# Sharing two groups of convolution channels between VectorE and ACT with GpSimd, tap by tap, in a two-layer speech encoder

## The chip, the cores and the metric

The kernel runs on one core of a Trainium2 chip. The metric is the device time of one execution in microseconds; the median of several runs is compared. A core has five engines that run their own queues in order and wait for each other through semaphores: TensorE (PE in the profile, its weight loads PEld), VectorE (DVE), ScalarE (ACT), GpSimd (POOL) and SyncE (SP), which here issues most of the transfers.

## The reference

Two layers of a Conformer-like block over 512 tokens of 1024 features, in float32. Each layer is a half-step feed-forward block, a mixing block, a second half-step feed-forward block and a norm:

```python
x = x + 0.5 * swiglu(rms_norm(x, ffn1_norm[l]), ...)
h = rms_norm(x, mix_norm[l])
p = h @ w_in[l]
attn = mla_group(p[..., :o_kv], p[..., o_kv:o_pe], p[..., o_pe:o_cv], ...)
conv = conv_group(p[..., o_cv:], conv_w[l], conv_b[l], conv_ln_g[l], conv_ln_b[l])
x = x + jnp.concatenate([attn, conv], axis=-1) @ w_out[l]
x = x + 0.5 * swiglu(rms_norm(x, ffn2_norm[l]), ...)
x = rms_norm(x, post_norm[l])
```

The attention has 8 heads with low-rank queries and keys and a block-causal mask. The convolution is the part that matters here; it has 512 channels, and each channel has a filter of its own with 31 taps over time:

```python
def conv_group(u_raw, conv_w, conv_b, ln_g, ln_b):
    a, g = u_raw[..., :CONV_W], u_raw[..., CONV_W:]
    u = a * jax.nn.sigmoid(g)
    y = lax.conv_general_dilated(u, conv_w[:, None, :], window_strides=(1,), padding=[(CONV_K - 1, 0)],
                                 feature_group_count=CONV_W)   # causal, depthwise
    y = y + conv_b
    return jax.nn.silu(layer_norm(y, ln_g, ln_b))              # norm over the 512 channels of a token
```

## The kernel before

Features lie on the 128 partitions and the 512 tokens along the free dimension, so the 512 convolution channels are four groups of 128, `c` = 0 to 3, each a tile of 128x512. A product of matrices is done as three matmuls of rounded parts (`mm3`, L153 to L157: high by high, high by low, low by high). The high part of a weight tile is a copy on ACT (L138) and the low part a subtraction on VectorE (L144); for the output weights `wo` of kind "sum" the low part is a copy of the negative on ACT (L141) and a transfer from GpSimd's queue that adds onto it (L142). `split` (L159) makes the two parts of an activation tile, the high one on ACT (L161), the low one on VectorE (L162).

The program is written in an order of its own, and a planner orders the instructions of each engine at build time by a timeline of its own (`schedule_with_timeline_sim=True`, L1237); the queues then run in that fixed order, however long things take. `tc.issue_after(i)` keeps an instruction behind `i` in that order.

`mix_body` (L617) is the mixing block. Its projections run on TensorE in the order of `SEQ` (L44): the inputs of channel group 0 come first, those of group 1 (`c1`) after the first part of the queries, those of groups 2 and 3 (`c2`, `c3`) last, behind the keys. `glu` (L624) forms `u[c]` out of them (VectorE L626, L630, L632, ACT L628). Queries and keys get their norms with a power on GpSimd (`rsqrt`, L173: `scq` for queries, `sck` for keys; `order["keys"]` is the last of the keys' four). Attention then goes head by head through `STAGES` (L889): transposes of queries and keys (L811 to L818), scores with their maxima on VectorE (L836) and exponentials on ACT (L840), transposes of the probabilities (L855, evicted at L858), sums and values (L870, L877), the product with the reciprocal sum (L880) and, per pair of heads, the split into `at`.

The convolution is written behind attention (L914 to L933), but its instructions are put between those of attention and of the projections. Before, a letter a group says who does it (`CONV = "DAAD"`, L41):

- "D", groups 0 and 3: an accumulator `acc` in PSUM (tag `cv`, one bank, so one group at a time) is started by ACT (L918, the newest tap and the bias), VectorE adds the 30 other taps, one instruction each (L922), and ACT copies the result back over `u[c]` (L932).
- "A", groups 1 and 2: an accumulator `ys[c]` in SBUF is started by ACT; for each of the 30 other taps ACT makes the product `pr` (L926, three buffers) and GpSimd adds it to the accumulator (L930). Additions with `s >= PAUSE` (16), and all of group 2, come behind `order["keys"]`.

Then follows the norm over channels: GpSimd sums the four groups into `ysum` (L944 to L946), a matmul with a constant tile averages over the channels (L948, `pm`), VectorE subtracts that mean from each group (L954), squares and sums follow (ACT L184 and L187, VectorE L191), a matmul adds the squares over channels (L198), GpSimd takes the power (L173), a matmul spreads the result (L217, `pr`), and VectorE and ACT scale, apply silu and split (L964, L966, L161, L162) into `cv`.

The output product has eight row blocks `m`, each a sum of four products with `at` and four with `cv` in one PSUM bank. The `at` part of the first three blocks (`early_groups`, 36 matmuls) needs no convolution and lies in the program behind the squares; the `cv` part of these three, and then the other blocks, follow at L970 to L980, behind which the second feed-forward block begins.

Tiles: `kept` (tag `m`, 12 buffers) holds the four `u`, the four value tiles and the first two `at` pairs; the other two pairs come from the ring of 35 buffers.

Of the kernel before, what the change touches and what calls it, by code (L numbers as in the profile page):

```python
# [7 lines left out]
FP = mybir.dt.float32  # L8
# [3 lines left out]
AF = mybir.ActivationFunctionType  # L12
ALU = mybir.AluOpType
AX = mybir.AxisListType

P = 128
D = 1024
S = 512
# [11 lines left out]
CK = 31  # L30
# [6 lines left out]
WIDE = 6  # L37
NP = 3
NC = 2
CHUNKS = ((0, 2), (2, 5), (5, 8), (8, 11))  # L40
CONV = "DAAD"  # L41
AHEAD = 2
PAUSE = 16
SEQ = "q0 R c1 q1 q2 qo k kt tt uq uk c2 c3"  # L44
# [3 lines left out]
EARLY = "s"  # L48
PRELOAD = 1
E1 = 0  # L50
YP = 1
E2 = 2
E3 = 3
WOG = 3
# [20 lines left out]
def encoder_kernel(ctx: ExitStack, tc: tile.TileContext, xT, consts, vecs, rgain, wgu1, wd1, wdq1,  # L75
# [8 lines left out]
    psum = ctx.enter_context(tc.tile_pool(name="psum", bufs=7, space=PSUM))  # L84
    uid = [0]

    def nm(s):
        uid[0] += 1
        return f"{s}{uid[0]}"
# [4 lines left out]
    def tmp(w=S, dt=FP):  # L94
        return tmps.tile([P, w], dt, tag="t", name=nm("t"))

    def bank():
        return psum.tile([P, S], FP, tag="ps", name=nm("ps"))
# [4 lines left out]
    V, A, G, T = nc.vector, nc.scalar, nc.gpsimd, nc.tensor  # L103
# [26 lines left out]
    def vv(l, name):  # L130
        o, w = VOFF[name]
        return vec[:, l, o:o + w]
# [18 lines left out]
    order = {}  # L151
# [7 lines left out]
    def split(src, made=slot):  # L159
        hi, lo = made(FR), made(FR)  # L160
        order["high"] = A.copy(hi, src).ins  # L161
        order["evicted"] = V.tensor_tensor(lo, src, hi.bitcast(FP), ALU.subtract).ins  # L162
        return hi, lo
# [46 lines left out]
    def spread(r):  # L210

        dg = tmp()
        V.tensor_tensor(dg.rearrange("p (t j) -> p t j", t=NT),
                        ident[:, None, :].to_broadcast([P, NT, P]),
                        r[:, :, None].to_broadcast([P, NT, P]), ALU.mult)
        ps = bank()
        order["spread"] = T.matmul(ps, ones, dg, start=True, stop=True).ins  # L217
        return ps
# [13 lines left out]
    def groups(srcs, rhs, ws=None):  # L232

        ws = ws or [load_w(src, WC) for src in srcs]
        os = [bank() for _ in srcs]
        for ks in (range(KD - 1), range(KD - 1, KD)):
            for o, w in zip(os, ws):
                group(o, w, rhs, ks, KD)
        return os
# [373 lines left out]
    def mix(l, gx, norm, done):  # L613
        with tc.tile_pool(name="k", bufs=4) as kpool:
            mix_body(kpool, l, gx, norm, done)

    def mix_body(kpool, l, gx, norm, done):  # L617
        u, order = [], {}

        def kept(dt=FP):  # L620
            return kpool.tile([P, S], dt, tag="m", name=nm("m"), bufs=2 * WIDE)
        ys = [None if kind == "D" else kpool.tile([P, S], FP, tag="y", name=nm("y"), bufs=2) for kind in CONV]

        def glu(pa, pg):  # L624
            tg = tmp()
            V.tensor_tensor(tg, pg, R, ALU.mult)  # L626
            sg = tmp()
            order["gate"] = A.activation(sg, tg, AF.Sigmoid).ins  # L628
            ta = tmp()
            V.tensor_tensor(ta, pa, R, ALU.mult)  # L630
            uc = kept()
            (G if GLUP else V).tensor_tensor(uc, ta, sg, ALU.mult)  # L632
            u.append(uc)
# [155 lines left out]
        first = groups([wcv[l, 0], wcv[l, 1]], gx)  # L789
# [12 lines left out]
        at = []  # L802
# [3 lines left out]
        heads = [{} for _ in range(H)]  # L806
# [76 lines left out]
        def turn_out(h):  # L883

            if h % 2 == 0:
                return
            at.append(split(heads[h]["o"], kept if len(at) < 2 else slot))

        STAGES = [({"t": turn, "s": scores, "p": turn_p, "v": values, "o": turn_out}[c], int(d)) for c, d in zip(ORDER[::2], ORDER[1::2])]  # L889

# [5 lines left out]
        with tc.issue_after(order["turned"]):  # L896
            for t in range(NT):
                ps = up_kv(wv, t)
                v = kept()
                V.tensor_scalar(v, ps, sk[:, t:t + 1], None, ALU.mult)  # L900
                vs.append(v)
        with tc.issue_after(order["gate"]):
            scores(0)
        for step in range(H + 6):
            for stage, lag in STAGES:
                h = step - lag
# [4 lines left out]
        with tc.issue_after(order["keys"]):  # L911
            wo = [load_w(wout[l, m], WC, "sum") for m in range(WOP)]
        cw, cb = vv(l, "cw"), vv(l, "cb")
        for c in range(4):  # L914
            kind = CONV[c]
            acc = psum.tile([P, S], FP, tag="cv", name=nm("cv"), bufs=1) if kind == "D" else ys[c]
            tap = lambda k: cw[:, c * CK + k:c * CK + k + 1]
            A.activation(acc, u[c], AF.Identity, scale=tap(CK - 1), bias=cb[:, c:c + 1])  # L918
            for k in range(CK - 2, -1, -1):
                s = CK - 1 - k  # L920
                if kind == "D":
                    V.scalar_tensor_tensor(acc[:, s:], u[c][:, :S - s], tap(k), acc[:, s:], ALU.mult, ALU.add)  # L922
                    continue
                pr = kpool.tile([P, S], FP, tag="pr", name=nm("pr"), bufs=3)
                if kind == "A":
                    A.activation(pr[:, s:], u[c][:, :S - s], AF.Copy, scale=tap(k))  # L926
                else:
                    G.tensor_scalar(pr[:, s:], u[c][:, :S - s], tap(k), None, ALU.mult)
                with tc.issue_after(order["keys"]) if s >= PAUSE or c > 1 else nullcontext():
                    order["conv"] = G.tensor_tensor(acc[:, s:], acc[:, s:], pr[:, s:], ALU.add).ins  # L930
            if kind == "D":
                A.copy(u[c], acc)  # L932
                ys[c] = u[c]  # L933
        early = []

        def early_groups(ms):
            with tc.issue_after(heads[H - 1][EARLY]):
                for m in ms:
                    early.append(bank())
                    group(early[m], wo[m], at, range(4), KD)  # L940

        early_groups(range(E1))
        ysum = tmp()
        G.tensor_tensor(ysum, ys[0], ys[1], ALU.add)  # L944
        G.tensor_tensor(ysum, ysum, ys[2], ALU.add)
        (G if YP else V).tensor_tensor(ysum, ysum, ys[3], ALU.add)  # L946
        pm = bank()
        T.matmul(pm, onesm, ysum, start=True, stop=True)  # L948
        if PRELOAD:
# [8 lines left out]
        pr = spread(r)  # L958
        early_groups(range(E3, WOG))
        lg, lb = vv(l, "lg"), vv(l, "lb")  # L960
        cv = []
        for c in range(4):
            z = tmp()
            V.tensor_tensor(z, ys[c], pr, ALU.mult)  # L964
            s = tmp()
# [275 lines left out]
```

## Time and profile before

| what | value |
|---|---|
| median of 3 runs | 1813.45 us (1812.57 to 1814.0) |
| profiled execution, its own time | 1813.8 us |
| its span, first to last instruction | 1812.0 us |
| mean granted TensorE clock | 0.995 |
| ACT busy | 1095.9 us (60%) |
| GpSimd (POOL) busy | 424.4 us (23%) |
| convolution taps of layer 0, first to last | 372.8 to 505.5 us of the span |
| convolution taps of layer 1 | 1270.6 to 1405.9 us |

In a row of a timeline the first number is the start in us from the span's beginning, the second the time the row covers in us, then engine, line, operation, the tile written and the tiles read, the shapes, and the number of instructions that the row merges; in brackets stand the idle time of the engine ahead of the row and what ended it. Rows of the table of waits give total us, number of waits and the longest. Rows of windows give, after the window and its length, the busy us of each engine with its number of instructions, then the granted clock, the busy share of the DMA engines and GB/s. A row of one source line gives the duration in ns as minimum, median and maximum. The recorded durations of neighbouring instructions on one engine overlap a little, so a busy time can reach the window's full length.

### The profile page before, as it was taken

The numbers are of one execution on the slowest core, as the hardware profiler recorded it, in microseconds if no ns is written. First come the engines' busy times: TensorE is split into PE (matmuls) and PEld (weight loads), VectorE is DVE, ScalarE is ACT, GpSimd is POOL, SyncE is SP. The second block draws the span as 40 slices with busy tenths as digits, with TensorE's granted clock in tenths as the row PEclk, the third lists the DMA queues.
The fourth block names the chain that finished last, engine by engine and source line by source line (L and its number), as shares of the span: only waits on it lengthen the run. The fifth ranks groups of instructions, "written<-read, shape, count | busy, mean of one in ns | idle before, by whom it ended". The sixth has DMA issues, their size and how long they took to land. (4 is left out here: it accounts for less than half of the span.)

```text
span 1812.0 us, 29094 instructions
## 1 busy us (share of the span) xinstructions
PE 1777.8 (98%) x11238; PEld 1582.1 (87%) x11238; DVE 1496.1 (83%) x2263; ACT 1095.9 (60%) x1729; POOL 424.4 (23%) x343
## 2 busy tenths in 40 slices
PE   9999999999989999999999999999999899999998
PEld 7899999888668899999888999998976788999997
DVE  7898988689946989898779989876999569989884
ACT  5565656467943575756645656554779435656564
POOL 1000000258843000000310000002688420000102
PEclk9999999999999999999999999999999999999999
DMA  5657574325103466665426575743260126575752
GB/s 167 165 135 190 125 183 114 108 88 140 24 16 107 121 165 160 153 156 133 123 64 169 127 188 124 191 108 115 74 152 1 37 86 165 135 180 134 177 121 73
DMA packets 70411, 226.14 MB, mean 125 GB/s; under 512 B 7936, under 2 KB 8320, under 8 KB 70272
## 3 DMA queue, kind: packets, MB, share of 16 engines
q1 hardware_dynamic: 54000, 169.74, 29.9%
q0 software_dynamic: 16128, 54.53, 17.6%
q8 instruction: 88, 1.44, 0.3%
q14 instruction: 51, 0.42, 0.1%
q10 hardware_dynamic: 144, 0.00, 0.0%
HBM read 222.15 MB, written 2.10 MB: 124 GB/s over the span
## 5 line engine op out<-in xcount | busy, mean ns | idle before, releaser
L155 PE MATMUL ps<-r,wh 128*128 128x256 f32 (+1 forms) x2540 | 806.1, 318 | 0.0
L154 PE MATMUL ps<-r,wh 128*128 128x256 f32 (+1 forms) x2540 | 803.4, 320 | 2.4 <-ACT wh L1060 0.9
L156 PE MATMUL ps<-r,wl 128*128 128x256 f32 (+1 forms) x2348 | 750.5, 321 | 1.9 <-DVE wl L246 1.9
L154 PEld LDWEIGHTS ps<-r,wh 128*128 128x128 f32 x2540 | 481.0, 189 | 45.0 <-ACT wh L138 3.1
L155 PEld LDWEIGHTS ps<-r,wh 128*128 128x128 f32 x2540 | 482.0, 190 | 34.3 <-issue 1.4
L156 PEld LDWEIGHTS ps<-r,wl 128*128 128x128 f32 x2348 | 445.2, 190 | 37.4 <-DVE wl L246 3.5
L373 PE MATMUL ps<-xj,wh 128*128 128x512 f32 x864 | 304.8, 392 | 4.6 <-DVE t L426 4.6
L138 ACT CAST wh<-raw 128x1024 fp32r<-128x1024 f32 (+3 forms) x148 | 131.8, 899 | 201.1 <-PE ps L155 101.8
L390 POOL DMA_DIRECT2D ls<-in_wgu x72 | 62.6, 869 | 733.0 <-ACT ls L389 640.2
L244 ACT CAST wh<-fr 128x1024 fp32r<-128x1024 f32 (+1 forms) x160 | 157.8, 986 | 109.4 <-DVE fr L410 47.8
L144 DVE TENSOR_TENSOR wl<-raw,wh 128x1024 fp32r<-128x1024 f32 (+3 forms) x132 | 145.3, 1108 | 83.2 <-ACT wh L138 82.7
L246 DVE TENSOR_TENSOR wl<-fr,wh 128x1024 fp32r<-128x1024 f32 (+1 forms) x160 | 182.8, 1142 | 20.5 <-ACT wh L244 20.5
L373 PEld LDWEIGHTS ps<-xj,wh 128*128 128x128 f32 x864 | 161.3, 188 | 36.3 <-DVE t L426 6.2
L930 POOL TENSOR_TENSOR y<-y,pr 128x511 f32<-128x511 f32 (+14 forms) x120 | 160.8, 1340 | 56.2 <-ACT pr L926 49.0
L374 PE MATMUL ps<-xj,ls 128*128 128x256 f32 x576 | 161.3, 280 | 0.0
L246 DVE TENSOR_TENSOR wl<-raw,wh 128x1024 fp32r<-128x1024 f32 (+1 forms) x100 | 113.8, 1138 | 14.8 <-ACT wh L244 14.4
L244 ACT CAST wh<-raw 128x1024 fp32r<-128x1024 f32 (+1 forms) x100 | 98.1, 981 | 44.9 <-PE ps L155 27.9
L191 POOL TENSOR_TENSOR r<-r,t 128x512 f32<-128x512 f32 x45 | 75.1, 1678 | 175.7 <-ACT t L187 174.9
L389 ACT ACTIVATE ls<-fr 128x1024 fp32r<-128x1024 f32 (+1 forms) x56 | 56.1, 1001 | 88.3 <-PE ps L374 49.6
L374 PEld LDWEIGHTS ps<-xj,ls 128*128 128x128 f32 x576 | 108.3, 188 | 0.2
L926 ACT ACTIVATE pr<-m,vec 128x511 f32<-128x511 f32 (+14 forms) x120 | 87.1, 752 | 11.3 <-POOL y L930 11.3
L390 POOL DMA_DIRECT2D ls<-in_wdq x32 | 27.6, 862 | 269.7 <-ACT ls L389 269.7
(241 smaller groups left out, 2967.4 us busy)
## 6 DMA issues: line engine op xcount, KB each, us to landing
fr<-in_wgu SPq DMA_DIRECT2D x112, 512.0 KB, 4.2
ls<-in_wgu POOLq DMA_DIRECT2D x72, 512.0 KB, 6.8
raw<-in_wgu SPq DMA_DIRECT2D x62, 512.0 KB, 5.1
fr<-in_wdq SPq DMA_DIRECT2D x48, 384.0 KB, 5.4
ls<-in_wdq POOLq DMA_DIRECT2D x32, 384.0 KB, 4.7
raw<-in_wd SPq DMA_DIRECT2D x32, 384.0 KB, 3.1
raw<-in_wd SPq DMA_DIRECT2D x32, 256.0 KB, 2.7
raw<-in_wcv SPq DMA_DIRECT2D x16, 512.0 KB, 3.6
```

Source lines behind the costliest of these rows:

```text
L138: order["cast"] = A.copy(hi[:, :w], raw[:, :w]).ins
L144: (G if kind in POOLW.split() else V).tensor_tensor(lo[:, :w], raw[:, :w], hi[:, :w].bitcast(FP), ALU.subtract)
L154: T.matmul(o, lh, rh, start=first, stop=False, skip_group_check=free)
L155: T.matmul(o, lh, rl, start=False, stop=False, skip_group_check=free)
L156: order["mm"] = T.matmul(o, ll, rh, start=False, stop=last, skip_group_check=free).ins
L244: A.copy(hi[:, :w], src[:, :w])
L246: order["lo"] = V.tensor_tensor(lo[:, :w], src[:, :w], hi[:, :w].bitcast(FP), ALU.subtract).ins
L373: T.matmul(o, w[0][:, c], both, start=start and k == 0, stop=False, skip_group_check=True)
L374: last = T.matmul(o[:, 0:HS], w[1][:, c], both[:, 0:HS], start=False, stop=k == 3, skip_group_check=True).ins
L390: G.dma_start(out=lo[:, :n], in_=w, accum_op=ALU.add)
L926: A.activation(pr[:, s:], u[c][:, :S - s], AF.Copy, scale=tap(k))
L930: order["conv"] = G.tensor_tensor(acc[:, s:], acc[:, s:], pr[:, s:], ALU.add).ins
```

## The change

`CONV` is replaced by `TAPS = (14, 17, 31, 0)`: for group `c` with `n = TAPS[c]`, the taps at distances 0 to n − 1 go to ACT and GpSimd in the SBUF accumulator `ys[c]`, the taps at distances n to 30 to VectorE in the PSUM accumulator `acc`. Group 2 stays wholly with ACT and GpSimd, group 3 wholly with VectorE; groups 0 and 1, which were whole on either side, are shared. Where a group is shared, ACT starts both accumulators (the PSUM one with the product of distance n) and VectorE joins them with one addition. The sum of the four groups moves from GpSimd to VectorE, one addition as each group is done, the last one reading group 3 in PSUM. The additions of distances below 16 of groups 0 and 1 are free to come ahead of the keys; distance 16 of group 1 and all of group 2 stay behind them. The second pair of attention outputs moves from `kept` (now 10 buffers) to the ring, and tag `y` has three buffers instead of two.

```diff
-CONV = "DAAD"
+TAPS = (14, 17, 31, 0)
...
-            return kpool.tile([P, S], dt, tag="m", name=nm("m"), bufs=2 * WIDE)
-        ys = [None if kind == "D" else kpool.tile([P, S], FP, tag="y", name=nm("y"), bufs=2) for kind in CONV]
+            return kpool.tile([P, S], dt, tag="m", name=nm("m"), bufs=10)
+        ys = [kpool.tile([P, S], FP, tag="y", name=nm("y"), bufs=3) if n else None for n in TAPS]
...
-            at.append(split(heads[h]["o"], kept if len(at) < 2 else slot))
+            at.append(split(heads[h]["o"], kept if len(at) < 1 else slot))
...
-        for c in range(4):
-            kind = CONV[c]
-            acc = psum.tile([P, S], FP, tag="cv", name=nm("cv"), bufs=1) if kind == "D" else ys[c]
+        ysum = None
+        for c, n in enumerate(TAPS):
             tap = lambda k: cw[:, c * CK + k:c * CK + k + 1]
-            A.activation(acc, u[c], AF.Identity, scale=tap(CK - 1), bias=cb[:, c:c + 1])
-            for k in range(CK - 2, -1, -1):
-                s = CK - 1 - k
-                if kind == "D":
-                    V.scalar_tensor_tensor(acc[:, s:], u[c][:, :S - s], tap(k), acc[:, s:], ALU.mult, ALU.add)
+            acc = psum.tile([P, S], FP, tag="cv", name=nm("cv"), bufs=1) if n < CK else None
+            first = dict(func=AF.Identity, scale=tap(CK - 1), bias=cb[:, c:c + 1])
+            if n:
+                A.activation(ys[c], u[c], **first)
+            for s in range(n or 1, CK):
+                k = CK - 1 - s
+                if s == n:
+                    A.activation(acc[:, s:], u[c][:, :S - s], AF.Copy, scale=tap(k))
                     continue
+                if s == 1 and not n:
+                    A.activation(acc, u[c], **first)
+                V.scalar_tensor_tensor(acc[:, s:], u[c][:, :S - s], tap(k), acc[:, s:], ALU.mult, ALU.add)
+            for s in range(1, n):
+                k = CK - 1 - s
                 pr = kpool.tile([P, S], FP, tag="pr", name=nm("pr"), bufs=3)
-                if kind == "A":
-                    A.activation(pr[:, s:], u[c][:, :S - s], AF.Copy, scale=tap(k))
-                else:
-                    G.tensor_scalar(pr[:, s:], u[c][:, :S - s], tap(k), None, ALU.mult)
+                A.activation(pr[:, s:], u[c][:, :S - s], AF.Copy, scale=tap(k))
                 with tc.issue_after(order["keys"]) if s >= PAUSE or c > 1 else nullcontext():
-                    order["conv"] = G.tensor_tensor(acc[:, s:], acc[:, s:], pr[:, s:], ALU.add).ins
-            if kind == "D":
+                    order["conv"] = G.tensor_tensor(ys[c][:, s:], ys[c][:, s:], pr[:, s:], ALU.add).ins
+            if not n:
                 A.copy(u[c], acc)
                 ys[c] = u[c]
+            elif n < CK:
+                V.tensor_tensor(ys[c][:, n:], ys[c][:, n:], acc[:, n:], ALU.add)
+            if c:
+                last, ysum = ysum or ys[0], ysum or tmp()
+                V.tensor_tensor(ysum, last, ys[c] if n else acc, ALU.add)
...
-        ysum = tmp()
-        G.tensor_tensor(ysum, ys[0], ys[1], ALU.add)
-        G.tensor_tensor(ysum, ysum, ys[2], ALU.add)
-        (G if YP else V).tensor_tensor(ysum, ysum, ys[3], ALU.add)
         pm = bank()
         T.matmul(pm, onesm, ysum, start=True, stop=True)
```

More of the change, by code (lines that the diff above doesn't have):

```diff
@@ L50 @@
 E1 = 0
-YP = 1
 E2 = 2
```

## The prediction

> **What bounds the kernel now.** The page first, for the engine that carries the time, then the table of waits.
>
> ```profile
> span 1812.0 us, 29094 instructions
> ...
> PE 1777.8 (98%) x11238; PEld 1582.1 (87%) x11238; DVE 1496.1 (83%) x2263; ACT 1095.9 (60%) x1729; POOL 424.4 (23%) x343
> ```
> ```profile
> PEld ps L948 <- POOL t L946: 11.5, 2, 6.4
> ...
> ACT pr L926 <- POOL y L930: 11.3, 10, 2.0
> ...
> PE ps L948 <- POOL t L946: 11.0, 2, 6.1
> ```
>
> TensorE is busy for 1777.8 of 1812.0 us, so an elementwise change can win only where TensorE stops or crawls. Its longest named stop is at L948, the matmul that averages the convolution over its channels: two stops, one a layer, 11.0 us together, both ended by GpSimd's last addition of `ysum`. The windows around these two places come next.
>
> ```profile
> core 0: us, PE busy (x) PEld busy (x) DVE busy (x) ACT busy (x) POOL busy (x), PEclk, DMA share, GB/s
> ...
> 380.00:400.00 20.00, 20.00 (x125) 18.44 (x124) 18.99 (x25) 12.45 (x20) 15.55 (x11) 1.00 0.31 93
> ...
> 460.00:480.00 20.00, 18.87 (x125) 12.35 (x124) 19.84 (x41) 20.00 (x52) 16.59 (x15) 1.00 0.04 7
> 480.00:500.00 20.00, 18.77 (x138) 12.25 (x138) 19.04 (x37) 19.74 (x50) 18.89 (x15) 1.00 0.01 2
> 500.00:520.00 20.00, 15.16 (x85) 10.88 (x82) 9.00 (x13) 7.90 (x13) 9.25 (x7) 0.83 0.00 1
> ...
> 1390.00:1410.00 20.00, 12.80 (x103) 8.39 (x101) 11.00 (x20) 13.31 (x28) 17.67 (x14) 0.91 0.00 1
> ```
>
> During attention (460 to 500) VectorE, ACT and GpSimd are all nearly full; TensorE's small matmuls fit between. In 500 to 520 VectorE and ACT drop to half and the granted clock falls to 0.83. The timelines show who is late, GpSimd first, then VectorE and ACT, then TensorE.
>
> ```profile
> 383.98 5.80 POOL L930 TENSOR_TENSOR y<-y,pr 128x511 f32<-128x511 f32 x4 [20.30 <-ACT pr L926]
> ...
> 416.71 1.64 POOL L173 TENSOR_TENSOR scq<-ssh,minus_half 128x8 f32<-128x8 f32 x1 [2.08 <-DVE ssh L750]
> 421.09 3.88 POOL L173 TENSOR_TENSOR scq<-ssh,minus_half 128x8 f32<-128x8 f32 x1 [2.75 <-DVE ssh L750]
> ...
> 427.16 2.54 POOL L173 TENSOR_TENSOR scq<-ssh,minus_half 128x8 f32<-128x8 f32 x1 [1.05 <-DVE ssh L750]
> ...
> 438.79 0.89 POOL L142 DMA_DIRECT2D wl<-in_wout  x1
> 439.44 1.53 POOL L930 TENSOR_TENSOR y<-y,pr 128x496 f32<-128x496 f32 x1
> ...
> 477.05 28.42 POOL L930 TENSOR_TENSOR y<-y,pr 128x502 f32<-128x502 f32 x21 [0.40 <-ACT pr L926]
> 505.44 1.26 POOL L944 TENSOR_TENSOR t<-m,y 128x512 f32<-128x512 f32 x1
> ...
> 508.44 1.26 POOL L946 TENSOR_TENSOR t<-t,m 128x512 f32<-128x512 f32 x1
> ```
> ```profile
> 371.29 0.69 DVE L632 TENSOR_TENSOR m<-t,t 128x512 f32<-128x512 f32 x1 [0.78 <-ACT t L628]
> ...
> 498.01 0.71 DVE L922 SCALAR_TENSOR_TENSOR cv<-m,vec,cv 128x482 f32<-128x482 f32 x1
> ...
> 1395.54 0.71 DVE L922 SCALAR_TENSOR_TENSOR cv<-m,vec,cv 128x482 f32<-128x482 f32 x1
> ```
> ```profile
> 372.02 0.78 ACT L918 ACTIVATE cv<-m,vec 128x512 f32<-128x512 f32 x1 [0.28 <-DVE m L632]
> ...
> 501.32 0.70 ACT L926 ACTIVATE pr<-m,vec 128x482 f32<-128x482 f32 x1 [0.15 <-POOL y L930]
> ```
> ```profile
> 509.76 2.08 PE L948 MATMUL ps<-t,onesm 128*128 128x512 f32 x2 [4.84 <-POOL t L946]
> ...
> 514.62 0.63 PE L155 MATMUL ps<-r,wh 128*128 128x512 f32 x1
> 515.05 0.63 PE L156 MATMUL ps<-r,wl 128*128 128x512 f32 x1
> ...
> 519.03 0.95 PE L198 MATMUL ps<-ones,r 128*128 128x1 f32 x8
> ...
> 522.70 1.02 PE L217 MATMUL ps<-t,ones 128*128 128x512 f32 x2
> ...
> 526.63 1.20 PE L154 MATMUL ps<-r,wh 128*128 128x512 f32 x4
> ...
> 528.13 0.40 PE L155 MATMUL ps<-r,wh 128*128 128x512 f32 x1
> 528.36 0.39 PE L156 MATMUL ps<-r,wl 128*128 128x512 f32 x1
> ...
> 1408.59 2.08 PE L948 MATMUL ps<-t,onesm 128*128 128x512 f32 x2 [6.14 <-POOL t L946]
> ...
> 1424.94 1.19 PE L154 MATMUL ps<-r,wh 128*128 128x512 f32 x4
> ```
>
> VectorE has its last tap behind it at 498.72 (498.01 + 0.71). GpSimd, which ran its last 21 taps without a pause, is done with them at 505.5 and with `ysum` at 509.70. TensorE waits from 504.92 (509.76 − 4.84), and afterwards starts matmuls 0.43 us apart (514.62 to 515.05) against 0.23 later (528.13 to 528.36). The output products over the convolution's channels start at 526.63. The second layer is alike and worse: VectorE done at 1396.25, `ysum` awaited until 1408.59, output products at 1424.94. So GpSimd's late end is what binds in this stage, and its cause lies far ahead: it stood idle for 20.30 us before 383.98, because its first group needs `u[1]`, while `u[0]` was there at 371.98 (371.29 + 0.69).
>
> **The change part by part.** Counts first.
>
> ```profile
> L922 DVE SCALAR_TENSOR_TENSOR cv<-m,vec,cv x120: 672/731/755, 372.8 to 1395.5; 128x511 f32<-128x511 f32 x4, 128x510 f32<-128x510 f32 x4, 128x509 f32<-128x509 f32 x4, 128x508 f32<-128x508 f32 x4
> ...
> L930 POOL TENSOR_TENSOR y<-y,pr x120: 1204/1257/2090, 384.0 to 1404.2; 128x511 f32<-128x511 f32 x4, 128x510 f32<-128x510 f32 x4, 128x509 f32<-128x509 f32 x4, 128x508 f32<-128x508 f32 x4
> ...
> L926 ACT ACTIVATE pr<-m,vec x120: 690/726/897, 383.2 to 1401.2; 128x511 f32<-128x511 f32 x4, 128x510 f32<-128x510 f32 x4, 128x509 f32<-128x509 f32 x4, 128x508 f32<-128x508 f32 x4
> ```
>
> A layer has 60 taps on each side now. With (14, 17, 31, 0) GpSimd gets 13 + 16 + 30 = 59, VectorE 16 + 13 + 0 + 30 = 59. Hardly any work changes sides; it changes time.
>
> *GpSimd early.* Its first tap can follow `u[0]` (371.98), one ACT start of the accumulator (0.78) and one product (0.73): about 373.5, against 383.98, so 10.5 us sooner. The additions that need not wait for the keys rise from 15 to 13 + 15 = 28. At the pace of the unbroken stretch, 28.42 / 21 = 1.353 us a tap, the 13 extra ones need 17.6 us. The earlier start gives 10.5, the idle gaps in front of the three `scq` rows 2.08 + 2.75 + 1.05 = 5.9; so 1.2 us is left, which can push the keys' `rsqrt`, queued behind on GpSimd, and with it the start of attention.
>
> *GpSimd late.* After 439.44 it has 31 taps instead of 45: 31 × 1.353 = 41.9, plus four DMA issues of 0.65 (438.79 to 439.44), 2.6: done about 484 instead of 505.5. It leaves the path, with 14 us to spare; its three `ysum` additions go too.
>
> *VectorE.* Less 1 tap, plus two joins of the accumulators and three sums for `ysum`. No such join is in the trace; the nearest row is the 128x512 TENSOR_TENSOR of 371.29, 0.69. The first join lies near 391, in the window 380 to 400, where TensorE is busy for 20.00 of 20 us on projections whose operands are there: taken as nothing; without that cover it is 0.69. The second join must wait for a tap held until after the keys, so it and the three sums fall into the full attention stretch: 4 × 0.69 = 2.76 us. `ysum` is then complete at 498.72 + 2.76 = 501.5 and 1396.25 + 2.76 = 1399.0, that is 8.3 us before 509.76 and 9.6 before 1408.59.
>
> [...]
>
> ```profile
> 481.68 1.16 DVE L162 TENSOR_TENSOR m<-t,m 128x512 fp32r<-128x512 f32 x1
> ...
> 526.70 0.69 DVE L162 TENSOR_TENSOR r<-t,r 128x512 fp32r<-128x512 f32 x1
> ```
>
> [...]
>
> *ACT.* One product fewer and one copy out of PSUM fewer, two accumulator starts more: near zero by the 0.73 of L926. But 14 of its products leave the attention stretch, 14 × 0.73 = 10 us of an engine that shows 20.00 of 20. I count nothing for that, because VectorE (19.84, 19.04) stays full.
>
> *New waits.* VectorE now waits for GpSimd at both joins and at the sum over `ys[2]`; behind each wait its in-order queue holds the casts of weights, the maxima and evictions of attention. How late GpSimd can be against the fixed order: its last tap ends 3.4 us after ACT's last product (505.47 against 502.02), and in the `ysum` wait it was 4.84 and 6.14 late. Below, a join can cost nothing; it cannot gain. I take 0.5 us a layer for all three, near zero because GpSimd should be 14 us ahead at the last one, and keep 6.14 each for the range.
>
> *Buffers.* One pair of attention outputs moves to the ring, `m` shrinks by two, `y` grows by one. No row has a wait on that tile of the ring; nothing taken.
>
> *The tail.* From the L948 matmul to the output products there are 16.87 us (526.63 − 509.76) and 16.35 now. The clock loss in it should go (TensorE no longer stands), but attention's last evictions will share VectorE with it; I leave it unchanged. TensorE's own floor: from 504.92, 36 early products at 0.23 (8.3), L948 and the spread 1.02 each, the sums 0.95: 516.2, earlier than 526.63 − 8.3 = 518.3, so the floor does not bind.
>
> Sum: 8.3 + 9.6 = 17.9, less 2 × 1.2 for late keys and 2 × 0.5 for joins: 14.5 us. The profiled execution took 1813.8 us, 1.8 outside its span; 1799.3 remains. The median of the runs is 0.35 below the profiled one, so 1799 us.
>
> **The rivals.** Same sign, more: the tail shrinks with the full clock and only TensorE's floor binds, 516.2 for 526.63 and (1402.45 + 11.3 =) 1413.75 for 1424.94. That is 21.6 us, 1792. Against it: attention's end still uses VectorE.
>
> Same sign, less: one wait per layer inside attention costs what the old one did, 4.84 and 6.14. Then 17.9 − 11.0 = 6.9 us remain, about 1806.5. For it: ACT already waits for GpSimd ten times (11.3 us), so GpSimd runs behind the order it is given.
>
> No change: the order puts VectorE's taps of the last group behind attention's, so they end at about 505 and `ysum` again near 509: 1813.5. Against it: in the trace the taps are strewn evenly through attention.
>
> Slower: VectorE stands at two of its new waits in each layer (the second join at about 441 and the sum over `ys[2]` in mid-attention), each 4.84 and 6.14. That is 9.7 and 12.3, plus the 1.2 of late keys: 24.4 against 17.9, a loss of 6.5 us, 1820. It decides once the waits of a layer exceed 8.3 and 9.6. For it: the stretch has no slack on VectorE, so every wait there is paid in full. Against it: GpSimd's load after the keys falls by a third.
>
> **How the numbers follow.** Main case 0.42, more 0.15, less 0.20, no change 0.09, slower 0.14. Faster by over 0.2% (3.6 us, about what a measurement of this kernel can tell from no change) is 0.42 + 0.15 + 0.20 = 0.77; within it 0.09; slower 0.14. The range runs from just under the TensorE floor, 1790, up to no change, 1814, and leaves out the slower case and a little at the lower end.
>
> **What would show it.** Right: GpSimd's first tap near 373.5 and its last near 484; L948 waits for VectorE or not at all, starting near 501.5; the clock in the 20 us after it back at 1.00; the output products of layer 0 near 518. Wrong: idle time of VectorE in front of the joins or sums, released by GpSimd; `scq` or `sck` later than now; taps of the last group that end after 505; or VectorE's end of attention moved out by more than 3 us.

## The result, and the profile after

The changed kernel takes 1813.91 us (median of 12 runs, 1811.83 to 1818.81) against 1811.88 (12 runs, 1809.98 to 1814.0) for the kernel before on the same chip: a ratio of 1.0014, with an interval of 1.0005 to 1.0023. That is 2.0 us slower, inside the 0.2% that was called no change, where 1799 was forecast; it lies at the upper end of the range. The profiled execution is the quickest of the twelve, with an own time of 1811.83 us (span 1810.0), 2.1 under the median; differences of 2 us between two single profiles therefore mean nothing, and below only shifts of several us, or ones that return in several kernels, are used. Source lines of the changed kernel differ from those before by a few: taps on VectorE are L927, GpSimd's additions L933, the join L938, the sums L941, the channel mean L952, the maxima L835, attention's output product L879.

The page of the changed kernel, then its table of waits for TensorE (total us, number, longest):

```profile
span 1810.0 us, 29098 instructions
...
PE 1777.9 (98%) x11238; PEld 1585.2 (88%) x11238; DVE 1502.8 (83%) x2271; ACT 1099.6 (61%) x1729; POOL 411.9 (23%) x335
```
```profile
PE ps L952 <- DVE t L941: 6.9, 2, 3.5
...
PE ps L714 <- ACT r L678: 4.3, 2, 2.2
```

The stop at the channel mean, 11.0 us in two places before, is 6.9 us now and VectorE ends it instead of GpSimd. Another one is new: 4.3 us in two places at L714, in the projections, where TensorE had no stop; the granted clock over 400 to 410 is 0.69 there, 1.00 before. The windows show where the load went:

```profile
400.00:420.00 20.00, 17.86 (x93) 17.47 (x92) 19.45 (x37) 17.48 (x51) 18.81 (x18) 0.83 0.26 77
...
480.00:500.00 20.00, 19.52 (x137) 12.85 (x136) 19.28 (x38) 15.87 (x44) 10.53 (x9) 1.00 0.00 1
500.00:520.00 20.00, 16.54 (x110) 11.73 (x108) 13.39 (x24) 9.25 (x18) 0.00 (x0) 0.91 0.01 2
1390.00:1410.00 20.00, 16.54 (x134) 10.60 (x130) 15.82 (x30) 10.75 (x25) 0.00 (x0) 1.00 0.00 1
```

GpSimd does nothing at all in the two stretches in which it used to be late (500 to 520 and 1390 to 1410), and is full (18.81 of 20) in 400 to 420. VectorE stays full in 480 to 500 (19.28, before 19.04). GpSimd's own timeline:

```profile
373.87 17.30 POOL L933 TENSOR_TENSOR y<-y,pr 128x511 f32<-128x511 f32 x11 [10.44 <-ACT pr L931]
...
436.42 7.93 POOL L172 TENSOR_TENSOR sck<-ssk,minus_half 128x8 f32<-128x8 f32 x4 [1.68 <-DVE ssk L777]
...
482.09 9.43 POOL L933 TENSOR_TENSOR y<-y,pr 128x488 f32<-128x488 f32 x7 [0.44 <-ACT pr L931]
```

Its first tap starts at 373.87 (forecast 373.5) and its last ends at 491.52 (forecast 484). The keys' power is late, at 436.42 (429.67 before), and it waits there for VectorE. VectorE from the first maximum of attention to the sums, with the same first maximum in the kernel before ahead of it (453.68), and then TensorE after:

```profile
453.68 0.75 DVE L836 TENSOR_REDUCE mx<-ps 128x1 f32<-128x128 f32 x2
```
```profile
458.45 0.75 DVE L835 TENSOR_REDUCE mx<-ps 128x1 f32<-128x128 f32 x2
...
500.71 0.72 DVE L927 SCALAR_TENSOR_TENSOR cv<-m,vec,cv 128x482 f32<-128x482 f32 x1
...
501.67 0.68 DVE L161 TENSOR_TENSOR r<-t,r 128x512 fp32r<-128x512 f32 x1
...
508.52 0.69 DVE L879 TENSOR_TENSOR t<-ps,t 128x512 f32<-128x512 f32 x1 [1.65 <-PE ps L876]
509.12 0.68 DVE L941 TENSOR_TENSOR t<-y,y 128x512 f32<-128x512 f32 x1
...
511.12 0.68 DVE L941 TENSOR_TENSOR t<-t,cv 128x512 f32<-128x512 f32 x1
```
```profile
511.86 1.13 PE L952 MATMUL ps<-t,onesm 128*128 128x512 f32 x2 [3.46 <-DVE t L941]
...
527.53 1.19 PE L153 MATMUL ps<-r,wh 128*128 128x512 f32 x4
...
1409.23 1.12 PE L952 MATMUL ps<-t,onesm 128*128 128x512 f32 x2 [3.46 <-DVE t L941]
...
1423.31 1.19 PE L153 MATMUL ps<-r,wh 128*128 128x512 f32 x4
```

Two things stand out. Attention starts 4.8 us later (458.45 against 453.68; 5.2 in the second layer). And the last tap on VectorE is done at 501.43, all of GpSimd's ten us before that, yet the first of three sums starts only at 509.12, right behind attention's last output product. So the channel mean is at 511.86, later than before (509.76), and TensorE has stood still for 3.46 us since 508.40.

### The profile page after: what moved, and what is told of

It is laid out like the page before. It is cut to its first block, busy times and chain, and to the rows that moved or that the text cites. A ratio compares the mean times of both kernels' runs of the same rounds, so it can differ in the third digit from the quotient of the medians.

```text
span 1810.0 us, 29098 instructions
## 1 busy us (share of the span) xinstructions
PE 1777.9 (98%) x11238; PEld 1585.2 (88%) x11238; DVE 1502.8 (83%) x2271; ACT 1099.6 (61%) x1729; POOL 411.9 (23%) x335
## 3 DMA queue, kind: packets, MB, share of 16 engines
q0 software_dynamic: 16128, 54.53, 17.6%
## 5 line engine op out<-in xcount | busy, mean ns | idle before, releaser
L933 POOL TENSOR_TENSOR y<-y,pr 128x511 f32<-128x511 f32 (+29 forms) x118 | 160.9, 1368 | 32.6 <-ACT pr L931 26.4
L931 ACT ACTIVATE pr<-m,vec 128x511 f32<-128x511 f32 (+29 forms) x118 | 85.7, 738 | 15.4 <-POOL y L933 15.0
L927 DVE SCALAR_TENSOR_TENSOR cv<-m,vec,cv 128x493 f32<-128x493 f32 (+29 forms) x118 | 85.8, 727 | 4.2 <-ACT cv L923 2.9
```

The costliest lines, as they stand in the source:

```text
L933: order["conv"] = G.tensor_tensor(ys[c][:, s:], ys[c][:, s:], pr[:, s:], ALU.add).ins
```

## The experiments

Two questions: why do the sums come so late, and why does attention start late? For the sums, the first theory is the tile: `ysum` was written as one of five temporaries (`tmp()`), and attention's output products use the same five, so the sums wait until attention gives one back. The rival is that VectorE is simply full. For the late start, one theory is the new stop of TensorE near 402 with the lower clock behind it (ACT holds a product that waits for GpSimd, and with it the squares that TensorE needs); the other is that GpSimd's additions, moved beside VectorE's casts and rotations of queries and keys, slow VectorE.

**The sum in a tile of its own.**

```diff
-                last, ysum = ysum or ys[0], ysum or tmp()
+                last, ysum = ysum or ys[0], ysum or kpool.tile([P, S], FP, tag="ysum", name=nm("ysum"), bufs=1)
```

> The changed kernel with one edit: ysum gets a tile of its own in the pool of the mixing block instead of one of the five shared temporaries. Theory T (the three sums come late because ysum finds no free temporary until attention has given its own back; in the changed kernel they start at 509.12, though group 0 and 1 were ready at 450.75 and group 2 at 491.5): the sums move ahead of attention's end, the channel-mean matmul of layer 0 starts near 505.5 instead of 511.86 without a wait, the output products near 521 instead of 527.5, and both layers give 12 us: about 1802. Rival V (VectorE is simply full, so sums that come earlier only push attention's own work back): the output products stay within 2 us of 527.5, total 1811 to 1814.

Measured: 1808.71 us (1806.52 to 1810.89, 11 runs) against 1812.15; ratio 0.9978 (0.9970 to 0.9987). VectorE's first and last sum, and TensorE around the mean:

```profile
450.53 1.07 DVE L941 TENSOR_TENSOR ysum<-y,y 128x512 f32<-128x512 f32 x1
...
505.68 0.68 DVE L941 TENSOR_TENSOR ysum<-ysum,cv 128x512 f32<-128x512 f32 x1
```
```profile
506.52 2.10 PE L876 MATMUL ps<-r,m 128*64 128x512 f32 x10
508.55 1.12 PE L952 MATMUL ps<-ysum,onesm 128*128 128x512 f32 x2
...
511.69 0.86 PE L876 MATMUL ps<-r,m 128*64 128x256 f32 x6
```

The first sum moves from 509.12 to 450.53, the last starts 5.4 us earlier, on a VectorE that is no emptier (busy for 27.16 us of 480 to 510, 26.39 in the changed kernel), and the mean needs no wait: it runs between attention's last value matmuls. So it was the tile, and this one line turns the loss of 2.0 us into a gain of 3.4. The 1802 that was expected is missed by 7, and the rival has a part in that: attention's last value matmuls end at 512.55 instead of 508.40, and the output products start at 524.60, 2.9 us earlier and not 6.5. Attention still starts late in it (first maximum at 459.32).

**Holding back ACT's products, so that TensorE doesn't stop near 402.** The products of group 1 from distance 6 on are kept behind ACT's squares of the latents; once with the sum's tile as in the change, once with its own.

```diff
+                order["latent"] = A.activation(j[:, :DR], pk[t][:, KVL:KW], AF.Square, accum_out=sspe[:, t:t + 1]).ins
...
+                with tc.issue_after(order["latent"]) if c == 1 and s >= 6 else nullcontext():
+                    A.activation(pr[:, s:], u[c][:, :S - s], AF.Copy, scale=tap(k))
```

> The changed kernel with one edit: ACT's products of group 1 from distance 6 on stay behind the evictions of the latent keys. Theory H (ACT stands behind GpSimd at a full product buffer for 2.41 us at 401.34, the latent keys' evictions queue behind it, TensorE stops for 2.14 us at 401.57 and then runs at half clock until 410.5; the queries' products end 4.5 us later than in the kernel before): the stop and the half clock go, attention starts about 4.5 us earlier in each layer, total about 1805. Rival V (VectorE's work bounds attention, and it has only moved): the stop goes, but the end of attention moves by less than 1.5 us a layer, total 1811 to 1814.

> Both edits of the two runs before. H and T together: no stop near 402, the channel mean near 501, the output products near 517 in layer 0, total about 1794. If only one of the two holds, its own number, 1802 or 1805. Rival V: 1809 or more.

Measured: 1823.04 us (1819.63 to 1825.89, 5 runs; ratio 1.0055, 1.0042 to 1.0067), and with the own tile 1816.7 (1815.31 to 1819.41, 11 runs; 1.0023, 1.0014 to 1.0032), both against 1812.15. In the first of them the stop near 402 is gone, the clock of that stretch is full (1.00 over 400 to 410), and a new stop stands further on:

```profile
425.32 0.50 PE L155 MATMUL ps<-r,wl 128*128 128x512 f32 x1 [2.85 <-DVE wl L143]
```

It waits for a weight cast on VectorE, and the first maximum comes at 461.86, 3.4 us later still. So taking away the stop and the lower clock does not bring attention's start back; what would is not shown by this run, which came out slower than any of the expected times. The own tile is again worth 6.3 us (1823.04 − 1816.7).

**The sharing without the moved sums.** The three sums go back to GpSimd, behind all groups, as before the change.

```diff
-            if c:
-                last, ysum = ysum or ys[0], ysum or tmp()
-                V.tensor_tensor(ysum, last, ys[c] if n else acc, ALU.add)
...
+        ysum = tmp()
+        for c in range(1, 4):
+            G.tensor_tensor(ysum, ysum if c > 1 else ys[0], ys[c], ALU.add)
```

> The changed kernel with the three sums back on GpSimd, in the place and with the temporary that they had before; only the sharing of groups 0 and 1 is left. By T the sums still wait for a temporary, so the channel mean of layer 0 starts at 511 to 514 and the total is 1813 to 1817. If instead the 2.8 us that the sums add to VectorE are what costs, the channel mean comes near 509 and the total is 1808 to 1810. The stop near 402 stays either way.

Measured: 1805.72 us (1804.89 to 1808.83, 5 runs) against 1812.15; ratio 0.9963 (0.9951 to 0.9976). It beats both kernels, and both expected outcomes (1813 to 1817 and 1808 to 1810). GpSimd's first sum and TensorE behind it:

```profile
502.92 1.28 POOL L950 TENSOR_TENSOR t<-y,y 128x512 f32<-128x512 f32 x1 [10.92 <-DVE r L161]
```
```profile
506.57 2.32 PE L876 MATMUL ps<-r,m 128*64 128x512 f32 x16
508.82 1.12 PE L952 MATMUL ps<-t,onesm 128*128 128x512 f32 x2
...
523.46 1.19 PE L153 MATMUL ps<-r,wh 128*128 128x512 f32 x4
```

Here too the sums wait for the temporary, 10.92 us, until VectorE has split the second pair of attention outputs (L161, done at 502.84; the layer's four splits start at 487.67, 502.16, 506.67 and 510.39). But GpSimd has nothing queued behind them, and the last ends at 506.92 (505.64 + 1.28), in time: the mean follows attention's last matmul without a wait. What binds now is attention's own end on TensorE, 508.8.

This also says how far the tile explains the changed kernel. There the same split is done at 502.35 (501.67 + 0.68), and VectorE stands idle for 2.77 us between then and 508.52 (0.63, 0.49 and 1.65, each for something else), but the first sum runs only at 509.12, without a wait in front of it. So the tile kept the sums from running before 502.35; the other 6.8 us are the place behind attention's last output product that the planner gave them in VectorE's fixed queue. With a tile of their own it placed them earlier; why it chose that place with the shared tile is not shown.

**The moved sums without the sharing.** The taps as before (groups 0 and 3 whole on VectorE, 1 and 2 whole on ACT and GpSimd), the sums on VectorE. Tag `y` has two buffers again, as before the change.

```diff
-TAPS = (14, 17, 31, 0)
+TAPS = (0, 31, 31, 0)
...
-        ys = [kpool.tile([P, S], FP, tag="y", name=nm("y"), bufs=3) if n else None for n in TAPS]
+        ys = [kpool.tile([P, S], FP, tag="y", name=nm("y"), bufs=2) if n else None for n in TAPS]
```

> The changed kernel with TAPS = (0, 31, 31, 0): no group is shared, group 0 is whole on VectorE and group 1 whole on GpSimd as in the kernel before; only the three sums are on VectorE. With the runs before it completes the square of the two parts (sharing alone measured 1805.7). If the parts simply add (changed kernel 1813.9, sharing 1805.7, before 1812.1), it takes 1812.1 + 8.2 = 1820. If the sums cost only where sharing lets them wait behind attention, then here, where GpSimd's last tap at 505 ends anyway after most of attention, three sums of 0.69 replace three of 1.37, and it takes 1809 to 1812.

Measured: 1808.96 us (1806.87 to 1810.41, 11 runs) against 1811.86; ratio 0.9981 (0.9972 to 0.9990).

```profile
508.91 2.08 PE L952 MATMUL ps<-t,onesm 128*128 128x512 f32 x2 [4.32 <-DVE t L941]
```

Attention starts as before (454.12), GpSimd is late as before (its last tap ends at 506.31), and the sums behind it end at 508.86 instead of 509.70. With this the square is complete, each against the kernel before on its chip: sums alone −2.9 us, sharing alone −6.4, both +2.0. The two parts do not add: together they miss their sum of −9.3 by 11 us, because sharing shifts attention back (the run after the next asks why), and the sums on VectorE then stand behind that late attention.

**The sharing with a tile of its own for the sum.**

```diff
-        ysum = tmp()
+        ysum = kpool.tile([P, S], FP, tag="ysum", name=nm("ysum"), bufs=1)
```

> Sharing alone with a tile of its own for ysum, on GpSimd. In the run without it the first sum waited 10.9 us, until VectorE's split of the third pair of heads gave a temporary back. By theory T the first two sums follow the last tap at 492, the third follows the copy of group 3 at about 502, so ysum is complete near 503.5 instead of 506.9; but the values of attention end at 508.9, so the channel mean moves little if it stands behind them in TensorE's queue (1804 to 1806), and by up to 4 us a layer if it comes in between (1798 to 1802).

Measured: 1805.7 us (1803.52 to 1808.23, 8 runs) against 1811.86; ratio 0.9970 (0.9959 to 0.9981), no different from the sharing alone, as one of the two expected outcomes had it. The last sum starts at 503.71 instead of 505.64, but TensorE comes to the mean no sooner (509.07 against 508.82), without a stop ahead of it in either: the sums were no longer late, so freeing them earlier buys nothing. (The pair whose split gives the temporary back is the second, not the third as the expectation has it.)

**Group 1's additions behind the keys.** On top of the sharing alone, additions of group 1 from distance 5 on are kept behind the keys, so that GpSimd is quiet beside the rotations.

```diff
-                with tc.issue_after(order["keys"]) if s >= PAUSE or c > 1 else nullcontext():
+                with tc.issue_after(order["keys"]) if s >= (PAUSE, 5, 0)[c] else nullcontext():
```

> Sharing alone (sums on GpSimd, 1805.7) with GpSimd's additions of group 1 from distance 5 on held behind the keys instead of from 16 on: 11 additions fewer on GpSimd between 400 and 440 of layer 0. Theory C (VectorE's instructions with two inputs in SBUF stand still while GpSimd adds: the 128x256 rope products of 0.41 us took up to 1.48, VectorE was busy for 88.5 instead of 82.0 us up to the last key, and attention starts 4.8 us later): the rope rows return to 0.41, the first maximum of layer 0 comes near 454.5 instead of 458.9, attention's values end near 505 instead of 508.9, and the total is 1798 to 1802, as long as GpSimd, now done near 500, stays ahead. Rival W (the late start comes from VectorE's waits for its second accumulator and its joins, ahead of 400): the first maximum stays within 1.5 us of 458.9 and the total within 1804 to 1808.

Measured: 1812.27 us (1809.01 to 1815.43, 11 runs) against 1811.86; ratio 1.0006 (0.9997 to 1.0015). The rotations of the queries on VectorE (L706 before, L705 later: busy us, mean ns) before, in the changed kernel and here:

```profile
L706 DVE TENSOR_TENSOR t<-q,tab 128x256 f32<-128x256 f32 x8 | 2.8, 417 | 0.0
```
```profile
L705 DVE TENSOR_TENSOR t<-q,tab 128x256 f32<-128x256 f32 x8 | 4.7, 648 | 0.0
```
```profile
L705 DVE TENSOR_TENSOR t<-q,tab 128x256 f32<-128x256 f32 x8 | 2.8, 414 | 0.0
```
```profile
453.88 0.90 DVE L835 TENSOR_REDUCE mx<-ps 128x1 f32<-128x128 f32 x2
...
506.61 0.72 DVE L927 SCALAR_TENSOR_TENSOR cv<-m,vec,cv 128x482 f32<-128x482 f32 x1
```

(The last fence is VectorE's timeline here.) The rotations are as quick as before, the keys' last step ends at 443.31 (before 443.38, changed kernel 450.17), and attention starts at 453.88, as before: taking GpSimd's additions away from that stretch gives the start back, as the slowing theory says. VectorE up to the keys' last step, in the changed kernel and here (its busy time is the third figure behind the window's length):

```profile
371.00:450.17 79.17, 76.26 (x390) 67.75 (x388) 73.50 (x114) 59.34 (x114) 70.14 (x53) 0.96 0.33 95
```
```profile
371.00:443.31 72.31, 70.16 (x375) 62.40 (x374) 65.48 (x113) 51.71 (x101) 56.88 (x41) 1.00 0.31 91
```

For the same work (114 and 113 instructions) VectorE is busy 8.0 us longer in the changed kernel and idle 1.2 us less, which is the whole 6.9 us by which the keys end later; ACT's load, which falls here too, would show as idle time. The eight rotations are 1.9 us of it; two kinds of short instructions with one tile and one column as inputs (L781, 3.6 us against 1.9, and L749, 2.4 against 0.9) are another 3.2. Why these are longer as well was not tried. Both of VectorE's new waits ahead of the keys are still there in this kernel (1.4 us for the start of the PSUM accumulator, 1.8 at the first join), so they are not what makes the keys late. Nor is it mainly the clock, which was full in this execution: in the first of the next two runs, with the same additions held, it was as low as in the changed kernel (0.67 and 0.69 over 400 to 410), and the keys end at 445.47. But the time is 6.5 us worse than that of the sharing alone, and the 1798 to 1802 that were expected are missed: the last tap on VectorE now starts at 506.61, GpSimd's last sum waits for it, and TensorE stops for 4.26 us ahead of the mean (509.40). The second join waits for GpSimd until 460.17, and the last group, which needs the one PSUM bank that group 1 holds until its join, has its first tap at 464.39 (456.9 in the sharing alone). This explains a part only: the profiled execution, 1809.01 us, is the quickest of the eleven, and against the sharing alone its output products are 1.7 us later in the first layer and 2.1 in the second; where the rest of the 6.5 us lies no trace shows.

**A second bank for the accumulators.** With two `cv` banks, the other PSUM tiles have six instead of seven; once on top of the run before, once on top of the sharing alone. (A tile of the later norms, which has the same tag, gets two banks as well.)

```diff
-    psum = ctx.enter_context(tc.tile_pool(name="psum", bufs=7, space=PSUM))
+    psum = ctx.enter_context(tc.tile_pool(name="psum", bufs=6, space=PSUM))
...
-            acc = psum.tile([P, S], FP, tag="cv", name=nm("cv"), bufs=1) if n < CK else None
+            acc = psum.tile([P, S], FP, tag="cv", name=nm("cv"), bufs=2) if n < CK else None
```

> The sharing with the sums back on GpSimd and group 1's additions from distance 5 on behind the keys, as in the run before, and now two PSUM banks for accumulators (six instead of seven for the other tiles). Theory 'one bank': with one bank the last group's accumulator started only after group 1's join (460.2), its first tap on VectorE at 464.4 and its last at 506.6, behind attention. With two banks the last group starts near 452, its last tap ends by 502, GpSimd's third sum no longer waits for ACT's copy, the channel mean starts at 505 to 507 in layer 0, and the time is 1804 to 1808 us. Rival 'VectorE is full': the taps are pushed behind attention's work whatever the bank, the last tap still ends after 505 and the time stays at 1811 to 1814. Rival 'six banks are too few': attention itself ends later, over 507 on TensorE, and the time is above 1812.

> The control: the sharing with the sums back on GpSimd, unchanged otherwise, with two PSUM banks for accumulators and six for the other tiles. Theory 'one bank': here the second join is at 448 already and the last group started at 456.9, when its inputs were there, so a second bank gives little: 1804 to 1807 us (1805.7 without it). Rival 'six banks are too few': 2 us or more above 1805.7, by stops of TensorE for a PSUM tile.

Measured: 1817.37 us (1814.64 to 1819.35, 8 runs; ratio 1.0031, 1.0021 to 1.0041) and 1814.94 (1811.71 to 1818.36, 10 runs; 1.0014, 1.0004 to 1.0024), both against 1811.75. VectorE in the first of the two:

```profile
454.72 2.33 DVE L631 TENSOR_TENSOR m<-t,t 128x512 f32<-128x512 f32 x1 [3.83 <-ACT t L627]
...
460.93 0.74 DVE L835 TENSOR_REDUCE mx<-ps 128x1 f32<-128x128 f32 x2
...
502.69 0.72 DVE L927 SCALAR_TENSOR_TENSOR cv<-m,vec,cv 128x482 f32<-128x482 f32 x1
```

With two banks the last group no longer waits for the join (its last tap starts 3.9 us earlier, at 502.69, although the join itself is at 465.3), as the bank theory has it. But the six other banks are too few: a new wait of 3.83 us stands at the last group's inputs, attention starts at 460.93 and ends on TensorE at 514.27. In the sharing alone the second bank brings a wait of 4.06 us at the same place, attention starts at 462.67, and the loss is over 9 us (1814.94 against 1805.72, the kernel before being 0.4 us apart on the two chips) with nothing gained. TensorE's stops at the scores, released by an exponential on ACT that reads earlier scores (L839), are 6.3 us there against 2.2 without the second bank. The rival of six banks won on the time.

**Fewer taps on VectorE.** The sharing alone with `TAPS = (14, 24, 31, 0)`: seven taps a layer go from VectorE to ACT and GpSimd, which is idle for 10.9 us at the end.

> Sharing alone with TAPS = (14, 24, 31, 0): VectorE has 7 taps fewer (4.5 us at 0.64 from start to start) around 400 to 414, GpSimd 7 more, all behind the keys. If VectorE's load up to the keys is what makes attention start late (theory C or W alike), the first maximum of layer 0 comes 3 to 5 us earlier than 458.9 and the total is 1798 to 1802. If TensorE's stop near 402 (ACT late with the latent keys) sets the start, nothing moves: 1805 to 1807.

Measured: 1807.4 us (1805.11 to 1809.86, 11 runs) against 1811.86; ratio 0.9979 (0.9970 to 0.9988), no better than without it. The first maximum is at 460.10, where 3 to 5 us earlier than 458.92 was expected of either theory. Counted from the product that makes `u[0]`, attention starts after 88.7 us in the first layer and 85.7 in the second, against 87.1 and 88.4 in the sharing alone and 82.4 in both with group 1's additions held: fewer taps on VectorE do not bring the start back. Group 1's join comes 11 us later (459.5 against 448.2), the last group's accumulator starts behind it at 462.2 instead of 456.1, and VectorE's last tap is at 506.3: the single bank again, as with group 1's additions behind the keys.

## Why the prediction was wrong

Wrong in direction: 14.5 us of gain were forecast and 2.0 of loss measured.

*GpSimd early and late: right, as far as GpSimd goes.* First tap 373.87 for 373.5, and it left the path; its last tap is at 491.52 for 484, still well before the end. The stop it caused is gone.

*The step that failed first: `ysum` "complete at 501.5".* The prediction set the sums directly behind VectorE's last tap and asked only what they cost there. VectorE's last tap is 2.7 us later than before (501.43), but the sums end at 511.80: 10.4 us behind it. The sums needed a place to write, and the code gives them one of five temporaries that attention uses; that keeps them back until 502.35, and the planner put them behind attention's last output product. The prediction went through the buffers that the diff names (`m`, `y`, the ring) and not through `tmp()`, on which a moved instruction depends as well. Its rival "no change" had the right outcome (`ysum` again near 509) with another cause: it put the taps late; the taps were not late, the sums were, so its 1813.5 is luck. The run with a tile of its own shows the choice of the temporary as the cause, worth 5.4 us (2.0 + 3.4); even there `ysum` is complete only at 506.36 (505.68 + 0.68), 4.9 us behind the forecast, since VectorE's last tap itself ends at 503.99.

*The term that was mis-sized: late keys, 1.2 us a layer.* Measured is 4.8 in the first layer. The prediction counted GpSimd's queue: 17.6 us of additional taps into 16.4 of early start and gaps. GpSimd did fill its gaps, but the row of `sck` waits for VectorE and not the other way round. What was missed is the price on VectorE, 8.0 us of longer instructions up to the keys' last step. The additions moved from the attention stretch, where VectorE mostly reads PSUM (its taps took 755 ns at most, before and after the change), to the projections, where it subtracts and rotates from SBUF with two inputs:

```profile
L706 DVE TENSOR_TENSOR t<-q,tab x16: 407/410/422, 413.3 to 1321.0; 128x256 f32<-128x256 f32 x16
```
```profile
L705 DVE TENSOR_TENSOR t<-q,tab x16: 410/414/1480, 417.0 to 1326.5; 128x256 f32<-128x256 f32 x16
```

Most take what they took, but the longest takes 1480 ns for 422: 1.06 us longer. It runs from 427.79 to 429.27, while GpSimd makes an addition (L933, 427.07 to 428.99). With the additions of group 1 held, the longest of the same eight takes 416 ns. Whether it is the place of the inputs that makes the difference, no run shows. Of the two splits of one shape (L162) that the prediction shows, the first, 1.16 us, ran while GpSimd was adding, the second, 0.69, while it was idle; no such difference was counted for the 13 additions that moved ahead of the keys. Nor was it for the sums, taken at 0.69 each: in the run with a tile of its own the first took 1.07 us and the last 0.68; in that of the moved sums alone the first took 1.54 from 505.32, while GpSimd's last taps ran (to 506.31), and the other two 0.69 and 0.68. The cover that the prediction named for the first join ("TensorE is busy for 20.00 of 20 us on projections") was true and beside the point: VectorE, at 18.57 to 18.99 of 20 between 380 and 440, had hardly more slack than during attention.

*The joins: about as taken.* 0.5 us a layer was the term. The first waits 1.75 us for GpSimd, the second nothing; but the run with group 1 behind the keys has the first wait too and starts attention on time, so it costs little. The slower rival (VectorE standing at joins and sums) did not occur.

*The tail, taken as unchanged, got shorter.* From the mean to the output products there are 15.67 us in the first layer and 14.08 in the second, and 14.64 and 14.66 in the sharing alone, against 16.87 and 16.35. TensorE doesn't stop ahead of it there, and the granted clock in 500 to 520 is 1.00 in the sharing alone, against 0.83 before.

*The floor.* The prediction let TensorE end attention at 504.92 as before. With the late start it ends at 508.4, although attention itself runs faster (49.95 us from its first maximum for 51.24). Where the mean comes between the last value matmuls, as with a tile of its own, attention ends later still (512.55). The sharing alone has its mean right behind attention, and its output products start at 523.46, 3.2 us earlier than before, not 8.3. So even without the temporary the forecast was not reached; 1805.7 us is the best that these runs show.

What stays open: how to have both, an attention that starts at 453.9 and convolution taps that end by 502. Keeping the additions away from the rotations brought the first and cost the second through the single bank; a second bank brought most of the second (503.40) and cost the first.

## What to carry to other kernels

When instructions move from one stretch to another, list for the new place not only the engine that runs them but the engine beside it whose instructions they lengthen (here the rotations on VectorE, 648 ns on the mean for 417), and every tile they write, temporaries included: a free engine is no use while the tile it must write is held by other work, or while its fixed order puts that work first. Of a change in two parts, measure each alone: here each part wins and both together lose, and the better kernel was half of the change. A wait that disappears is worth only the distance to the next thing that is late, here attention's own end on TensorE.

## What the runs showed of the hardware that was not expected

In these runs the clock behind a stop of TensorE doesn't follow from the length of the stop. In the first run with two banks the new stop at L714 is 2.17 us long in both layers of one execution. The stops, and the windows that hold them (the granted clock is the third number from the end):

```profile
403.04 0.44 PE L714 MATMUL ps<-cst,r 128*128 128x128 f32 x2 [2.17 <-ACT r L678]
...
1301.77 0.44 PE L714 MATMUL ps<-cst,r 128*128 128x128 f32 x2 [2.17 <-ACT r L678]
```
```profile
400.00:410.00 10.00, 7.59 (x33) 7.05 (x32) 6.98 (x18) 7.48 (x30) 4.89 (x6) 0.67 0.35 104
...
1300.00:1310.00 10.00, 7.99 (x51) 7.71 (x52) 8.50 (x23) 9.58 (x36) 2.08 (x3) 1.00 0.36 101
```

In the first layer the clock is 0.67 over the window, in the second 1.00. In the changed kernel both layers lose (0.69 and 0.66; 0.50 from 404 to 410 in the first), with group 1 behind the keys neither (1.00 and 1.00), all by stops of 2.14 to 2.17 us. What decides it was not tried, and no run shows it.
